# Gating and output projections of a decoder layer: five pairs of weight tiles by seven products in place of three, with weight sums made ahead in DRAM

## The chip, the core and the metric

The kernel runs on one core of one Trainium2 chip. TensorE (PE) multiplies, with weight loads (PEld) beside it; VectorE (DVE), ScalarE (ACT) and GpSimd (POOL) work on tiles in SBUF; SyncE (SP) and POOL issue the DMAs. The metric is the device time of one execution in microseconds.

## The reference

One decoder layer in float32 for 256 tokens (T) of width 2048 (D). Everything of size is a product of the 256 x 2048 activations with a weight matrix:

```python
h = RMSNorm_pre(x); p = h @ w_in    # columns: A (conv), B (spatial gate), C (attention), 3 x D merge gates
y = (g_A*A + g_B*B + g_C*C) @ w_o;  x = x + RMSNorm_post(y)
h = RMSNorm_pre(x); u = causal_dwconv3(h @ w_up)
x = x + RMSNorm_post((silu(u_g) * u_v) @ w_down)
```

The change touches the columns of `w_in` that give the third merge gate `g_C` ("gating", two blocks cp0 and cp1 of 1024 columns), and the first 1024 columns of `w_o` ("o").

## The kernel before, in words

A weight tile of 128 rows by 1024 columns is fetched by SP into one of five `wraw` buffers. ACT copies it, rounded, to `whi` (the "high part"), DVE subtracts to get `wlo` (the "low part"); each has a ring of four. Activations are kept as high and low parts too, 128 tokens by 128 rows. A product of an activation with 512 columns is three matmuls: high by high, high by low, low by high. So a plain tile (one k) takes two token halves x two column halves x 3 = 12 matmuls, and k runs over KT = 16 tiles of the 2048 rows.

In three places, gating cp0, gating cp1 and o, two k-tiles at a time are taken as a pair and multiplied by Strassen's scheme in Winograd's form: seven products in place of eight, from sums of the weights' four blocks and sums of the activations' four blocks. That is 21 matmuls in place of 24. `NG` is the number of such pairs per place, `REST` the plain k-tiles. `in_sevens` sets the order: two plain tiles, then the pairs with plain tiles between, then what plain tiles are left. `Seven.seven` makes the weight sums of a pair with half-tile operations on DVE (`tt` holds them), `Seven.combine` adds the side banks at the end. The activations' sums stand in `sh`; for gating they are made by `input_sums` from `hT` during the attention, for o by `sums4` from `mac`, transposed by PE (`pm`) in `mix_gen`.

The program has these stages, in this order: conv branch (`wf_a`), u, compressed keys (`kk`) and q projections; two branches (`branch`, four column blocks cb each) that form `mac`, with the attention worked off beside them; gating cp0, the C output `py` for cb 0 and 1, gating cp1, `py` for cb 2 and 3; o; the second half of the output projection; the feed-forward's up projection in 44 steps; the down projection in two halves (`Pair(0)`, `Pair(1)`) of 14 pairs and 16 plain tiles each. The down projection already takes weight sums that POOL makes ahead during the feed-forward, with DMAs from DRAM to DRAM, half of them adding into their target: two or four DMAs ("steps") a pair, 84 in all. Before the steps of a feed-forward step stands a copy of one column (`tick`) that makes POOL wait until the step's result is there.

The order of the work around the change is written out by hand: `fixed` chains operations on ACT and DVE each in the order of the code, `in_line` does so on PE; work outside these chains (attention, `mix_gen`, the adds to `mac`) is placed among them by the scheduler. In the down projection's second half, `keep` says after which pair a weight tile for the very end is prepared ahead into a buffer (`kept`) of the activations `gh` and `gl` that earlier pairs have read.

Of the kernel before, what the change touches and what calls it, by code (L numbers as in the profile page):

```python
# [43 lines left out]
NG, REST = 3, list(range(6, KT))  # L44
# [15 lines left out]
def block(ctx: ExitStack, tc: tile.TileContext, x, xf, fp, cst, rows, sgw, w1, w2, wf_a, wt_bv, wf_bu, wf_c,  # L60
# [473 lines left out]
    for j in range(8):  # L534
        pa = ftile(wf_a[2 * j], hT)
        sa = q1(f"sa{j}")
        fsum(pa, sa, rb=rb)
# [8 lines left out]
        pump(BUDGET)
# [44 lines left out]
    vbd = P1.tile([128, 2, 4, 128], F32, name="vbd")  # L591
# [280 lines left out]
    def input_sums(j):  # L872
# [3 lines left out]
        sums4(a[0], a[1], sh[:, j], f"h{j}")  # L876
        yield 0

    def attn():
# [3 lines left out]
        for n, u in enumerate(units):  # L883
# [3 lines left out]
            if n % 2 and n // 2 < NG:  # L887
                yield from input_sums(n // 2)
# [50 lines left out]
    class Seven:  # L939
# [23 lines left out]
        def seven(self, b, a, tt, acts, nm, last):  # L963

            L, U = slice(0, 512), slice(512, 1024)
            (hb, lb), (ha, la), (ht, lt), (h4, l4) = (ring(nm + x) for x in "bat4")
            high(hb, b)
            fixed(V, V.tensor_sub, tt[:, L], b[:, L], a[:, U])
            fixed(V, V.tensor_sub, a[:, U], a[:, U], a[:, L])
            high(ha, a)  # L970
            rest(lb, b, hb)
            fixed(V, V.tensor_sub, tt[:, U], b[:, L], a[:, U])
            high(ht, tt[:, 0:1024])
# [19 lines left out]
    def in_sevens(pr, plain, pairs, act, acts, tt, nm):  # L993
# [23 lines left out]
    def branch(bi, act_of):  # L1017

        for cb in range(4):
# [47 lines left out]
            for t in range(2):  # L1067
                for a in range(2):
                    cc = slice(cb * 512 + a * 256, cb * 512 + a * 256 + 256)
                    y = mac[:, t, cc] if bi == 0 else tgs[t, a]  # L1070
                    with tc.high_priority(offset=int(PR)):
                        V.scalar_tensor_tensor(y, tgs[t, a], 1.0, py[t][:, a * 256:a * 256 + 256], op0=ALU.add,
                                               op1=ALU.mult)
                        if bi:
                            V.tensor_add(mac[:, t, cc], mac[:, t, cc], y)
            pump(BUDGET)

    def mix_gen(cb):

        for j in range(2 * cb, 2 * cb + 2):  # L1080
# [10 lines left out]
            if j < NG:  # L1091
# [3 lines left out]
                mix["a", j] = a  # L1095
# [130 lines left out]
    def acts_m(j):  # L1226
        s1, s2, s4, s3 = parts(sh[:, j], range(4))
        return s4, m2(2 * j + 1, H1), m2(2 * j, H1), s1, s3, s2, m2(2 * j + 1, H2)

    in_sevens(po2, wt_op, wt_oq, m2, acts_m, tt, "o")  # L1230
# [179 lines left out]
    DR_seq = []  # L1410

    def pool_dma(*args, **kw):

        with ExitStack() as order:
            for ins in DR_seq:
                order.enter_context(tc.issue_after(ins))
            DR_seq[:] = [G.dma_start(*args, **kw).ins]  # L1417

    tick = PZ.tile([128, 1], F32, name="tick")
    ahead_of = {(p, j): DR.tile([128, 2 + n % 2, 512], F32, name=f"ahead{p}_{j}") for p in range(2)  # L1420
                for n, j in enumerate(TURNS[p])}
    away = [DR.tile([128, 2, 384], F32, name=f"away{j}") for j in range(AWAY)]

    def ahead_steps():

        late = deque()
        add = {"accum_op": ALU.add}
        for p in range(2):
            for n, j in enumerate(TURNS[p]):
                src, dst = wt_dq[p, j].rearrange("p (b n) -> p b n", b=4), ahead_of[p, j]  # L1430
                yield dst[:, 0:2], src[:, 2:4], {}
                if n % 2:
                    yield dst[:, 2], src[:, 0], {}
                while len(late) > 1 - n % 2:
                    yield late.popleft()
                late.append((dst[:, 0:2], src[:, 0:4:2], add))
                if n % 2:
                    late.append((dst[:, 2], dst[:, 1], add))
        yield from late

    steps = list(ahead_steps())
    count = len(steps)
    for i in range(NFT):
# [19 lines left out]
        for j, (k0, k1) in enumerate(PAIRS):  # L1463
            if i == k0:
                first = acc[0]
            elif i == k1:
# [3 lines left out]
                if j < AWAY:  # L1470
                    pool_dma(away[j], dst.rearrange("p x a b -> p x (a b)").bitcast(F32))
        with ExitStack() as order:
            for ins in DR_seq:
                order.enter_context(tc.issue_after(ins))
            DR_seq[:] = [G.tensor_copy(tick, g2(i, slice(0, 1))[0].bitcast(F32)).ins]
        while steps and len(steps) > count * (NFT - 2 - i) // (NFT - 2):
            dst, src, how = steps.pop(0)
            pool_dma(dst, src, **how)
# [15 lines left out]
    for j in TURNS[0][-AWAY:]:  # L1494
        pool_dma(home[:, j], away[j])
# [14 lines left out]
    class Pair(Seven):  # L1510
# [10 lines left out]
        def quad(self, n):  # L1521
# [3 lines left out]
            nm, last = f"q{self.p}_{j}", n == len(PAIRS) - 1  # L1525
            b = fetch(wt_dq[self.p, j][:, 0:1024], 1024)
            a = scratch()
            ahead = ahead_of[self.p, j]
            nc.sync.dma_start(a, ahead[:, 0:2].rearrange("p b n -> p (b n)"))
            r = fetch(wt_dq[self.p, j][:, 1536:2048], 512)  # L1530
            if n % 2:
                nc.sync.dma_start(r[:, 512:], ahead[:, 2])
            tt = fin[:, 7168:8192]
            s1, s2, s4 = summed_acts(j)
            L, U = slice(0, 512), slice(512, 1024)
            (hb, lb), (ha, la), (ht, lt), (hr, lr) = (ring(nm + x) for x in "batr")
            high(hb, b)
            if n % 2:
                rest(lb, b, hb)
                high(ha, a)  # L1540
                fixed(V, V.tensor_add, tt[:, L], b[:, U], r[:, U])
                rest(la, a, ha)
                high(hr, r)
                high(ht[:, L], tt[:, L])
                rest(lr, r, hr)
                rest(lt[:, L], tt[:, L], ht[:, L])
                six, four, one = ((hr, lr), U), ((ht, lt), L), ((hr, lr), L)
            else:
                fixed(V, V.tensor_add, tt[:, L], b[:, L], a[:, U])
                rest(lb, b, hb)  # L1550
                high(ha, a)
                fixed(V, V.tensor_add, tt[:, U], b[:, U], tt[:, L])
                rest(la, a, ha)
                high(ht, tt)
                high(hr[:, L], r[:, L])
                rest(lt, tt, ht)
                rest(lr[:, L], r[:, L], hr[:, L])
                six, four, one = ((ht, lt), L), ((ht, lt), U), ((hr, lr), L)
            todo = [(self.p6, s2, *six), (self.p1, g2(k0, H1), *one), (self.c[1][0], g2(k1, H2), *four)]
            side = (self.p1, self.p5, self.p6, self.p7)  # L1560
# [259 lines left out]
```

## Time and profile before

| what | value |
|---|---|
| runs | 1567.49, 1566.93, 1567.20 us; median 1567.2 |
| the profiled execution | 1566.37 us, span 1564.7, granted clock 0.998 |
| busy over the span | PE 1554.1, DVE 1284.4, ACT 925.3, POOL 112.7 us |
| conv, u, kk, q projections | 54 to 299 us |
| the two branches | 299 to 460, 460 to 622 |
| gating cp0, cp1 | 622 to 663, 686 to 728 |
| first half of the output projection | 751 to 794 |
| feed-forward, up | 840 to 1342 |
| down projection, two halves | 1342 to 1440, 1440 to 1555 |

All times are of one profiled execution on the one core, counted from the span's start. Busy time of PE overlaps: a matmul's row is longer than the distance to the next, since they are pipelined. The stages are read off the tiles that PE writes: `pg0a`, `pg1a`, `poa`, `pd0a`, `pd1a` and so on.

### The profile page before, as it was taken

What the parts mean: (1) busy time and instruction counts of PE and PEld (TensorE: products, weight loads), DVE (VectorE), ACT (ScalarE), POOL (GpSimd) and SP (SyncE); (2) the same over time, 40 slices, a digit from 0 to 9 for tenths busy, and PEclk for the clock granted to TensorE, in tenths of its full rate; (3) what the DMA queues carried; (4) which work ended last, traced back from release to release, by engine and by line L of the source; (5) the groups of instructions that cost most, each with busy time, mean ns of one, the idle gap of its engine ahead of it and who ended that gap; (6) DMA issues with size and microseconds to landing.
All of it is one profiled execution on the core that took longest, in us unless ns stands there. A gap on an engine that the chain in (4) does not pass through costs nothing.

```text
span 1564.7 us, 22800 instructions
## 1 busy us (share of the span) xinstructions
PE 1554.1 (99%) x8130; PEld 1320.0 (84%) x8130; DVE 1284.4 (82%) x2185; ACT 925.3 (59%) x1489; POOL 112.7 (7%) x182
## 2 busy tenths in 40 slices
PE   9999999999999999999999999999999999999998
PEld 7888889888887777888888888888888888888876
DVE  7899999978665554879887988888888777789997
ACT  7544544467487575556566656565555555566763
POOL 1000020000000000000000022122111121100000
PEclk9999999999999999999999999999999999999999
DMA  9555556657554546656684699889988899988793
GB/s 372 189 194 179 188 180 207 197 184 252 164 165 135 162 148 189 196 174 211 227 282 148 217 334 299 263 250 273 275 268 271 270 252 273 314 263 276 261 356 116
DMA packets 107442, 358.82 MB, mean 229 GB/s; under 512 B 11968, under 2 KB 13312, under 8 KB 106304
## 3 DMA queue, kind: packets, MB, share of 16 engines
q1 hardware_dynamic: 90144, 312.92, 60.2%
q0 software_dynamic: 16752, 44.05, 11.5%
q8 instruction: 63, 1.03, 0.3%
q10 hardware_dynamic: 432, 0.41, 0.1%
q14 instruction: 51, 0.42, 0.1%
HBM read 350.51 MB, written 42.47 MB: 251 GB/s over the span
## 4 chain that ended last, share of the span: by engine, by line
PE 97%; DVE 1%; ACT 1%; DMA 0%; issue 0%; DVEq 0%; SPq 0%; ACTq 0%
PE ps L178 29%; PE ps L185 15%; PE pd0b L953 5%; PE pg L199 4%; PE pg L200 4%; PE pg L198 4%; PE pd1a L953 3%; PE py L199 3%; PE py L198 3%; PE py L200 3%; PE pd0a L953 2%; PE pd1b L953 2%; PE poa L953 2%; PE pg1a L953 2%; PE pg0a L953 2%; PE po L198 1%
## 5 line engine op out<-in xcount | busy, mean ns | idle before, releaser
L150 DVE TENSOR_TENSOR wlo<-wraw,whi 128x1024 fp32r<-128x1024 f32 (+1 forms) x376 | 456.9, 1218 | 96.2 <-ACT whi L149 90.0
L149 ACT ACTIVATE whi<-wraw 128x1024 fp32r<-128x1024 f32 (+1 forms) x376 | 393.4, 1051 | 143.4 <-PE pg L200 42.0
L178 PE MATMUL ps<-h2T,whi 128*128 128x512 f32 x1360 | 325.0, 391 | 0.0
L178 PEld LDWEIGHTS ps<-h2T,whi 128*128 128x128 f32 x1360 | 249.8, 188 | 48.2
L185 PEld LDWEIGHTS ps<-h2T,wlo 128*128 128x128 f32 x1360 | 174.5, 191 | 6.7
L185 PE MATMUL ps<-h2T,wlo 128*128 128x256 f32 x1360 | 176.6, 283 | 0.0
L220 ACT ACTIVATE t<-ps 128x256 f32<-128x256 f32 x125 | 47.6, 382 | 186.3 <-PE ps L178 185.6
L178 PE MATMUL ps<-hT,whi 128*128 128x512 f32 x640 | 157.4, 392 | 0.0
L178 PEld LDWEIGHTS ps<-hT,whi 128*128 128x128 f32 x640 | 116.0, 188 | 21.3
L918 DVE TENSOR_TENSOR wlowraw<-wraw,whiwraw 128x1024 fp32r<-128x1024 f32 x74 | 89.7, 1223 | 34.1 <-ACT whiwraw L918 32.8
L481 DVE SCALAR_TENSOR_TENSOR cv<-hb,fps,cv 128x256 f32<-128x256 f32 x240 | 105.1, 479 | 0.2 <-ACT cv L477 0.2
L918 ACT ACTIVATE whiwraw<-wraw 128x1024 fp32r<-128x1024 f32 x74 | 77.8, 1058 | 46.3 <-PE py L200 16.5
L221 DVE TENSOR_TENSOR t<-ps,t 128x256 f32<-128x256 f32 x125 | 52.9, 424 | 63.3 <-ACT t L220 62.8
L200 PE MATMUL pg<-whi,hT 128*128 128x512 f32 x256 | 100.6, 393 | 0.0
L199 PE MATMUL pg<-wlo,hT 128*128 128x512 f32 x256 | 100.5, 393 | 0.0
L198 PE MATMUL pg<-whi,hT 128*128 128x512 f32 x256 | 98.7, 393 | 0.3 <-ACT mg L1042 0.3
L185 PEld LDWEIGHTS ps<-hT,wlo 128*128 128x128 f32 x640 | 84.7, 190 | 4.7
L185 PE MATMUL ps<-hT,wlo 128*128 128x256 f32 x640 | 86.8, 283 | 0.0
L199 PEld LDWEIGHTS pg<-wlo,hT 128*128 128x128 f32 x256 | 48.1, 188 | 10.4 <-issue 0.3
L200 PEld LDWEIGHTS pg<-whi,hT 128*128 128x128 f32 x256 | 48.1, 188 | 10.2 <-issue 0.7
L198 PEld LDWEIGHTS pg<-whi,hT 128*128 128x128 f32 x256 | 47.9, 188 | 10.0 <-ACT mg L1042 0.4
L1417 POOL DMA_DIRECT2D ahead<-in_wt_dq_dram x70 | 55.2, 814 | 6.5 <-DMA ahead<-in_wt_dq_dram 4.0
(1792 smaller groups left out, 2922.6 us busy)
## 6 DMA issues: line engine op xcount, KB each, us to landing
wraw<-in_wf_up_dram SPq DMA_DIRECT2D x176, 512.0 KB, 5.8
wraw<-in_wt_g_dram SPq DMA_DIRECT2D x64, 512.0 KB, 4.2
ahead<-in_wt_dq_dram POOLq DMA_DIRECT2D x56, 512.0 KB, 9.1
wraw<-in_wt_p_dram SPq DMA_DIRECT2D x48, 512.0 KB, 4.4
wraw<-in_wf_a_dram SPq DMA_DIRECT2D x32, 512.0 KB, 4.2
wraw<-in_wt_dn_dram SPq DMA_DIRECT2D x32, 512.0 KB, 4.8
wraw<-in_wt_dq_dram SPq DMA_DIRECT2D x28, 512.0 KB, 5.2
fin<-ahead SPq DMA_DIRECT2D x28, 512.0 KB, 5.1
```

Of the source, the lines that this page charges most:

```text
L149: S.activation(hi[:, :n], raw[:, :n], AF.Copy)
L150: V.tensor_sub(lo[:, :n], raw[:, :n], hi[:, :n].bitcast(F32))
L178: ins = PE.matmul(ps[:, :, ts], lhsT=ws[k // 8][0][:, c:c + 128], rhs=mov[:, k, :, ts], start=(k == 0 and not t), stop=(k == n - 1), skip_ ...
L185: ins = PE.matmul(ps[:, 1, ts], lhsT=ws[k // 8][1][:, c:c + 128], rhs=mov[:, k, 0, ts], start=False, stop=False, skip_group_check=True).ins
L198: PE.matmul(ps, lhsT=xh, rhs=hi, start=first, stop=False)
L199: PE.matmul(ps, lhsT=xh, rhs=lo, start=False, stop=False)
L200: return PE.matmul(ps, lhsT=xl, rhs=hi, start=False, stop=last).ins
L221: V.tensor_add(t1 if rb is not None else dst, ps[:, 0], t1)
L481: V.scalar_tensor_tensor(ca[:, j], hb[:, j, k:k + T], w(j, k), ca[:, j], op0=ALU.mult, op1=ALU.add)
L918: seq[eng] = [op(*args, **kw).ins]
L953: ins = PE.matmul(bank, lhsT=a[x], rhs=w[y], start=first and j == 0, stop=last and j == 2).ins
L1417: DR_seq[:] = [G.dma_start(*args, **kw).ins]
```

## The change

`NG` goes from 3 to 5 and `REST` from ten to six plain tiles, in all three places; between the pairs stand 0, 1, 0, 1, 0 plain tiles in place of 2, 2, 1. The pairs there now take their sums from DRAM in the way of the down projection, whose body becomes `Seven.seven`; the signs of the sums and of the final additions follow it. The 42 steps for these pairs stand first in a list of 126. `ahead_by` issues them: one after each of 8 conv, 8 u, 4 kk and 8 q tiles, and four after each column block of the two branches, 60 in all; 66 stay in the feed-forward. The activations' sums of pairs 3 and 4 get a buffer of their own, `sh2`; the fetched sums one of two halves, `qa` for gating and `oa` for o. In the last stage, `keep` is set after the pairs 5, 7, 11, 12 in place of 5, 7, 9, 11.

```diff
-NG, REST = 3, list(range(6, KT))
+NG, REST = 5, list(range(10, KT))
...
+    def ahead_steps():
+        quads = [(("g", cp, j), wt_gq[cp, j], j % 2) for cp in range(2) for j in range(NG)]
+        quads += [(("o", j), wt_oq[j], j % 2) for j in range(NG)]
+        quads += [((p, j), wt_dq[p, j], n % 2) for p in range(2) for n, j in enumerate(TURNS[p])]
+        for i, (key, _, six) in enumerate(quads):
+            made[key] = DR.tile([128, 2 + six, 512], F32, name=f"ahead{i}"), six
...
+        for key, src, six in quads:
+            src, dst = src.rearrange("p (b n) -> p b n", b=4), made[key][0]
+            yield dst[:, 0:2], src[:, 2:4], {}
+            if six:
+                yield dst[:, 2], src[:, 0], {}
+            while len(late) > 1 - six:
+                yield late.popleft()
+            late.append((dst[:, 0:2], src[:, 0:4:2], add))
+            if six:
+                late.append((dst[:, 2], dst[:, 1], add))
...
+    def ahead_by(mark, n):
+        pooled(G.tensor_copy, tick, mark)
+        for dst, src, how in steps[:n]:
+            pooled(G.dma_start, dst, src, **how)
+        del steps[:n]
...
+        ahead_by(hb[:, j, 30:31], 1)
...
+        ahead_by(ub[:, j, 0:1], 1)
...
+        ahead_by(kk[:, i % 2, i // 2, 0:1], 1)
...
+        ahead_by(qf[:, i, 0:1], 1)
...
+    for j in range(3, NG):
+        bg.append(input_sums(j))
...
-        def seven(self, b, a, tt, acts, nm, last):
+        def seven(self, quad, key, a, tt, acts, nm, last):
+            src, six = made[key]
+            b = fetch(quad[:, 0:1024], 1024)
+            nc.sync.dma_start(a, src[:, 0:2].rearrange("p b n -> p (b n)"))
+            r = fetch(quad[:, 1536:2048], 512)
+            if six:
+                nc.sync.dma_start(r[:, 512:], src[:, 2])
...
+            high(hb, b)
+            if six:
+                rest(lb, b, hb)
+                high(ha, a)
+                fixed(V, V.tensor_add, tt[:, L], b[:, U], r[:, U])
+                rest(la, a, ha)
+                high(hr, r)
+                high(ht[:, L], tt[:, L])
+                rest(lr, r, hr)
+                rest(lt[:, L], tt[:, L], ht[:, L])
...
+            else:
+                fixed(V, V.tensor_add, tt[:, L], b[:, L], a[:, U])
+                rest(lb, b, hb)
+                high(ha, a)
+                fixed(V, V.tensor_add, tt[:, U], b[:, U], tt[:, L])
+                rest(la, a, ha)
+                high(ht, tt)
+                high(hr[:, L], r[:, L])
+                rest(lt, tt, ht)
+                rest(lr[:, L], r[:, L], hr[:, L])
...
         for j in range(NG):
-            for _ in range((2, 2, 1)[j]):
+            for _ in range((0, 1, 0, 1, 0)[j]):
...
+            ahead_by(mac[:, 0, cb * 512:cb * 512 + 1], 4)
...
-                for j in range(NG):
-                    sums4(*mix["a", j], sh[:, j], f"m{j}")
+                for j in range(4):
+                    sums4(*mix["a", j], sh_of(j), f"m{j}")
...
-        keep = 1 if j in (5, 7, 9, 11) else 0
+        keep = 1 if j in (5, 7, 11, 12) else 0
```

How this moves instructions, at three places. First DVE at the start of o. Before, from the last C output's second low part (`wlowraw`) to the first pair's (`o0`) low parts:

```order
L918 TENSOR_TENSOR wlowraw_7119_7122<-wraw_7119,whiwraw_7119_7121 128x1024
L1155 SCALAR_TENSOR_TENSOR gates_6515<-gates_6515,py_6974 128x512
L1155 SCALAR_TENSOR_TENSOR gates_6515<-gates_6515,py_6975 128x512
L1156 TENSOR_TENSOR mac<-mac,gates_6515 128x512 x2
L918 TENSOR_TENSOR wlowraw_7137_7140<-wraw_7137,whiwraw_7137_7139 128x1024
L918 TENSOR_TENSOR tt<-wraw_7155,wraw_7157 128x512
L1088 SCALAR_TENSOR_TENSOR ml<-pm_6960,mh 128x512
L1088 SCALAR_TENSOR_TENSOR ml<-pm_6967,mh 128x512
L918 TENSOR_TENSOR wraw_7157<-wraw_7157 128x512
L918 TENSOR_TENSOR wloo0b<-wraw_7155,whio0b 128x1024
```

And after:

```order
L975 TENSOR_TENSOR wlowraw_7316_7319<-wraw_7316,whiwraw_7316_7318 128x1024
L975 TENSOR_TENSOR tt<-wraw_7346,oa 128x512
L975 TENSOR_TENSOR wloo0b<-wraw_7346,whio0b 128x1024
L925 TENSOR_TENSOR sh_5030<-sqm_7103,sh_5030 128x256
L1237 SCALAR_TENSOR_TENSOR gates_6704<-gates_6704,py_7200 128x512
L1237 SCALAR_TENSOR_TENSOR gates_6704<-gates_6704,py_7201 128x512
L975 TENSOR_TENSOR tt<-wraw_7346,tt 128x512
L975 TENSOR_TENSOR wloo0a<-oa,whio0a 128x1024
L1164 SCALAR_TENSOR_TENSOR ml<-pm_7172,mh 128x512
L1164 SCALAR_TENSOR_TENSOR ml<-pm_7193,mh 128x512
L1238 TENSOR_TENSOR mac<-mac,gates_6704 128x512 x2
L918 TENSOR_TENSOR spm_7183<-ma_7180,ma_7179 128x128
```

The additions to `mac` (L1156, now L1238) stood right behind `gates`; now two half-tile sums, a low part and both `ml` stand ahead of them, and the sums of pair 4's activations (`spm`) follow.

Second, ACT in the last stage, around pairs 9 and 0 of the down projection's second half. Before:

```order
L918 ACTIVATE whiq_9t<-fin 128x512
L918 ACTIVATE whiwraw_14688_14690<-wraw_14688 128x1024
L918 ACTIVATE kept_14706<-wraw_14707 128x1024
L918 ACTIVATE whiq_0b<-wraw_14711 128x1024
L918 ACTIVATE whiq_0a<-fin 128x1024
```

After, from the same pair on, and two pairs later:

```order
L975 ACTIVATE whiq_9t<-fin 128x512
L975 ACTIVATE whiwraw_14879_14881<-wraw_14879 128x1024
L975 ACTIVATE whiq_0b<-wraw_14897 128x1024
L975 ACTIVATE whiq_0a<-fin 128x1024
...
L975 ACTIVATE whiq_1t<-fin 128x512
L975 ACTIVATE whiwraw_14991_14993<-wraw_14991 128x1024
L975 ACTIVATE kept_15009<-wraw_15010 128x1024
L975 ACTIVATE whiq_2b<-wraw_15014 128x1024
```

The kept tile behind pair 9 is gone from there and stands behind pair 1; DVE's order has the same move.

Third, POOL's queue in the first branch. Before, the paddings of `bt` (the attention's compressed keys) stand one behind the other:

```order
L608 MEMSET bt_3536 128x16
L608 MEMSET bt_3579 128x16
L608 MEMSET bt_3855 128x16
L608 MEMSET bt_3860 128x16
L608 MEMSET bt_3865 128x16
```

After:

```order
L653 MEMSET bt_3643 128x16
L653 MEMSET bt_3686 128x16
L122 COPY tick<-mac 128x1
L122 DMA ahead_79<-in_wt_oq_dram 128x1024
L122 DMA ahead_78<-in_wt_oq_dram 128x2x512
L122 DMA ahead_80<-in_wt_oq_dram 128x1024
L122 DMA ahead_80<-in_wt_oq_dram 128x512
L653 MEMSET bt_3967 128x16
L653 MEMSET bt_3972 128x16
```

Between the two halves' paddings now stand a wait for `mac`'s second column block and four issues.

More of the change, by code (lines that the diff above doesn't have):

```diff
@@ L64, in block @@
     V, S, PE, G = nc.vector, nc.scalar, nc.tensor, nc.gpsimd
+    DR = ctx.enter_context(tc.tile_pool(name="dram", bufs=1, space=bass.MemoryType.DRAM))
     PZ = ctx.enter_context(tc.tile_pool(name="pz", bufs=1))
@@ L112, in block, with pooled @@
     fetched = [None]
+    in_pool = []
+    def pooled(op, *args, **kw):
+        with ExitStack() as order:
+            for ins in in_pool:
+                order.enter_context(tc.issue_after(ins))
+            in_pool[:] = [op(*args, **kw).ins]
+    tick = PZ.tile([128, 1], F32, name="tick")
+    made = {}
+    def ahead_steps():
[4 more added lines that the diff above has]
+            made[key] = DR.tile([128, 2 + six, 512], F32, name=f"ahead{i}"), six
+        late = deque()
+        add = {"accum_op": ALU.add}
+        for key, src, six in quads:
[8 more added lines that the diff above has]
+                late.append((dst[:, 2], dst[:, 1], add))
+        yield from late
+    steps = list(ahead_steps())
+    def ahead_by(mark, n):
[3 more added lines that the diff above has]
+        del steps[:n]
     def split2(raw):
@@ L590, in block @@
     kcb = P1.tile([128, 2, 32], F32, name="kcb")
-    vbd = P1.tile([128, 2, 4, 128], F32, name="vbd")
+    vbd = P1.tile([128, 2, 4, 128], F32, tag="vbd", name="vbd")
     kd_t = s8([128, 2, 4, T], F32, "kd")
@@ L855, in values, with sh_of @@
             yield 650
-    sh = P1.tile([128, NG, 2, 4, 128], R, name="sh")
+    sh = P1.tile([128, 3, 2, 4, 128], R, name="sh")
+    sh2 = []
+    def sh_of(j):
+        if j >= 3 and not sh2:
+            sh2.append(s8([128, 2, 2, 4, 128], R, "sh2"))
+        return sh[:, j] if j < 3 else sh2[0][:, j - 3]
     H1, H2 = slice(0, 128), slice(128, T)
@@ L886, in attn @@
             yield from u.weights()
-            if n % 2 and n // 2 < NG:
+            if n % 2 and n // 2 < 3:
                 yield from input_sums(n // 2)
@@ L965, in seven @@
             L, U = slice(0, 512), slice(512, 1024)
-            (hb, lb), (ha, la), (ht, lt), (h4, l4) = (ring(nm + x) for x in "bat4")
+            (hb, lb), (ha, la), (ht, lt), (hr, lr) = (ring(nm + x) for x in "batr")
             high(hb, b)
[L968 to L973, printed above, removed]
@@ L991, in combine, with total, in_sevens @@
             fixed(V, V.tensor_add, self.at(1, 0), self.p7, self.at(1, 0))
-    def in_sevens(pr, plain, pairs, act, acts, tt, nm):
+        def total(self, n):
+            return V.tensor_sub if n else V.tensor_add
+    def in_sevens(pr, plain, pairs, act, acts, keys, spare, tt, nm):
         todo = [(k, weights(plain[REST.index(k)])) for k in REST[0:2]]
@@ L998, in in_sevens @@
         for j in range(NG):
-            for _ in range((2, 2, 1)[j]):
+            for _ in range((0, 1, 0, 1, 0)[j]):
                 k = rest_.pop(0)
                 pr.k_tiles([(k, weights(plain[REST.index(k)]))], act)
-            b, a = (fetch(pairs[j][:, x:x + 1024], 1024) for x in (0, 1024))
-            pr.seven(b, a, tt, acts(j), f"{nm}{j}", j == NG - 1)
+            pr.seven(pairs[j], (*keys, j), spare(j), tt, acts(j), f"{nm}{j}", j == NG - 1)
         for k in rest_:
@@ L1109, in hx, with acts_of @@
         return hT[:, k, 0, ts], hT[:, k, 1, ts]
-    def acts_h(j):
-        s1, s2, s4, s3 = parts(sh[:, j], range(4))
-        return s4, hx(2 * j + 1, H1), hx(2 * j, H1), s1, s3, s2, hx(2 * j + 1, H2)
+    def acts_of(j, x):
+        s1, s2, s4, s3 = parts(sh_of(j), range(4))
+        return s4, x(2 * j + 1, H1), s3, s1, s2, x(2 * j + 1, H2), x(2 * j, H1)
     def wp(cb, k):
@@ L1121, in block @@
         gates = s8([128, 2, 2, 512], F32, f"gates{cp}")
+        pump(1e6)
         if cp == 0:
-            tt = s8([128, 2048], F32, "tt")
-        pump(1e6)
+            tt = P1.tile([128, 1024], F32, tag="vbd", name="tt")
+            qa = s8([128, 2, 1024], F32, "qa")
         pr = Seven([PS.tile([128, 512], F32, tag="acc", name=f"pg{cp}a{i}") for i in range(4)],
@@ L1131, in block @@
             for t in range(2):
-                fixed(V, V.tensor_add, gates[:, t, n], pr.c[t][n], gates[:, t, n])
+                fixed(V, pr.total(n), gates[:, t, n], pr.c[t][n], gates[:, t, n])
                 fixed(S, S.activation, gates[:, t, n], gates[:, t, n], AF.Tanh, scale=rh[:, t:t + 1])
@@ L1224, in m2 @@
         return mh[:, k, ts], ml[:, k, ts]
[L1226 to L1230, printed above, removed]
+    oa = P0.tile([128, 2, 1024], F32, tag="hT", name="oa")
+    in_sevens(po2, wt_op, wt_oq, m2, lambda j: acts_of(j, m2), ("o",), lambda j: oa[:, j % 2], tt, "o")
     for n in range(2):
@@ L1408, in kept_sums @@
         return (se, sf)[j % 10 // 5][:, :, j % 5]
[L1410 to L1421, printed above, removed]
-    away = [DR.tile([128, 2, 384], F32, name=f"away{j}") for j in range(AWAY)]
[L1424 to L1441, printed above, removed]
+    away = [DR.tile([128, 2, 384], F32, name=f"away{j}") for j in range(AWAY)]
     count = len(steps)
@@ L1470, in block @@
                 if j < AWAY:
[L1471 to L1478, printed above, removed]
+                    pooled(G.dma_start, away[j], dst.rearrange("p x a b -> p x (a b)").bitcast(F32))
+        ahead_by(g2(i, slice(0, 1))[0].bitcast(F32), max(0, len(steps) - count * (NFT - 2 - i) // (NFT - 2)))
     P2b_ctx.close()
@@ L1494, in block @@
     for j in TURNS[0][-AWAY:]:
-        pool_dma(home[:, j], away[j])
+        pooled(G.dma_start, home[:, j], away[j])
     def summed_acts(j):
@@ L1524, in quad @@
             k0, k1 = PAIRS[j]
[L1525 to L1533, printed above, removed]
-            s1, s2, s4 = summed_acts(j)
@@ L1535, in quad @@
[L1535 to L1558, printed above, removed]
@@ L1559, in quad @@
-            todo = [(self.p6, s2, *six), (self.p1, g2(k0, H1), *one), (self.c[1][0], g2(k1, H2), *four)]
-            side = (self.p1, self.p5, self.p6, self.p7)
-            for bank_, act, (h, l), c in (
-                    (self.c[0][1], s4, (hb, lb), L), (self.c[0][0], g2(k1, H1), (hb, lb), U),
-                    (self.p7, g2(k0, H2), (ha, la), L), (self.p5, s1, (ha, la), U),
-                    *(todo if n % 2 else [todo[0], todo[2], todo[1]])):
-                in_line(self.mm, bank_, act, (h[:, c], l[:, c]), last and any(bank_ is x for x in side))
@@ L1578, in at @@
+            self.seven(wt_dq[self.p, j], (self.p, j), scratch(), fin[:, 7168:8192],
+                       (s4, g2(k1, H1), g2(k0, H2), s1, s2, g2(k1, H2), g2(k0, H1)), f"q{self.p}_{j}",
+                       n == len(PAIRS) - 1)
         def at(self, t, n):
```

42 lines of the change are left out of this document (17 added, 25 removed).

## The prediction

> **What bounds the kernel now.** I read the page first: engine shares, then the chain of waits.
>
> ```profile
> PE 1554.1 (99%) x8130; PEld 1320.0 (84%) x8130; DVE 1284.4 (82%) x2185; ACT 925.3 (59%) x1489; POOL 112.7 (7%) x182
> PE 97%; DVE 1%; ACT 1%; DMA 0%; issue 0%; DVEq 0%; SPq 0%; ACTq 0%
> ```
>
> The chain runs through PE for 97% of the span, so a matmul removed is time removed, if what feeds PE keeps up. What one costs is read from the chain inside the first gating projection (start, length, count):
>
> ```profile
> 622.08 12.25 PE pg0a L953 x54
> 634.32 2.74 PE pg0b L953 x12
> 637.06 7.49 PE pg0a L953 x33
> ```
>
> That is 12.25 / 54 = 0.227 us per matmul of 512 columns. Single rows of the same matmul (below) read 0.39 us; they overlap, and pricing by them would almost double the gain. Next the stages (stretch, length, then busy time of PE, PEld, DVE, ACT, POOL, granted clock, DMA share, GB/s):
>
> ```profile
> 54.00:110.00 56.00, 56.00 (x324) 49.49 (x323) 54.00 (x100) 30.47 (x42) 0.00 (x0) 1.00 0.60 195
> 110.00:226.00 116.00, 116.00 (x675) 102.45 (x674) 113.90 (x224) 56.12 (x84) 8.46 (x16) 1.00 0.57 183
> 226.00:262.00 36.00, 36.00 (x261) 34.82 (x260) 35.62 (x67) 16.69 (x24) 0.00 (x0) 1.00 0.71 213
> 460.00:622.00 162.00, 162.00 (x793) 124.92 (x792) 84.99 (x180) 105.95 (x233) 0.57 (x1) 1.00 0.52 159
> 622.00:664.00 42.00, 42.00 (x187) 34.72 (x186) 36.52 (x47) 22.57 (x25) 0.00 (x0) 1.00 0.60 192
> 750.00:794.00 44.00, 44.00 (x203) 36.45 (x202) 39.60 (x49) 24.39 (x27) 1.08 (x2) 1.00 0.68 236
> 864.00:1342.00 478.00, 478.00 (x2738) 421.96 (x2737) 399.09 (x698) 282.79 (x464) 91.96 (x132) 1.00 0.90 271
> 1342.00:1440.00 98.00, 98.00 (x434) 81.16 (x433) 85.99 (x93) 65.69 (x69) 2.59 (x5) 1.00 0.87 289
> 1440.00:1509.00 69.00, 69.00 (x306) 57.13 (x305) 64.46 (x70) 47.74 (x56) 0.00 (x0) 1.00 0.83 283
> ```
>
> PE is full in each, and DVE is the engine nearest behind it. The third gating projection is the two stretches 622 to 664 and a twin at 686; 750 to 794 is the first half of the output projection.
>
> **Part 1: fewer matmuls.** A plain pair of weight tiles takes 24 matmuls, a pair by seven products 21. Two more pairs in each of three places: 3 x 2 x 3 = 18 fewer (the order has 4189 rows on PE before, 4171 after), 18 x 0.227 = **-4.1 us**, 1.4 us per place.
>
> **Part 2: DVE in those places.** Prices (busy sum, mean ns):
>
> ```profile
> L918 DVE TENSOR_TENSOR wlowraw<-wraw,whiwraw 128x1024 fp32r<-128x1024 f32 x9 | 10.8, 1221 | 2.4 <-ACT whiwraw L918 2.2
> L918 DVE TENSOR_TENSOR tt<-wraw,wraw 128x512 f32<-128x512 f32 x6 | 4.1, 684 | 0.0
> ```
>
> A pair before: 3.5 low parts and four half-tile sums, 3.5 x 1.22 + 4 x 0.68 = 7.0. After, with sums from DRAM: two half-tile sums, 5.6, or one, 5.0. A place goes from 10 x 1.22 + 3 x 7.0 = 33.2 to 6 x 1.22 + 3 x 5.6 + 2 x 5.0 = 34.1: +0.9. Gating: 36.52 + 0.9 = 37.4 in 40.6 us, 92%. The last stretch of the table runs the same cadence of pairs (two, then a plain tile) at 64.46 / 69 = 93% DVE with PE full, so I cost this at 0. The output half also gets the activation sums of one more pair (four 128x128 and two 128x256 additions, by the tile sizes an estimate of 2 us): 39.60 + 0.9 + 2 = 42.5 in 42.6. That has no cover in the stretch itself; the stretch's end is additions that PE doesn't wait for. Bounds 0 and +3 (all of it exposed); beyond the start (part 3) I take 0, as the row nearest in cadence had no wait. The sums of pairs 3 and 4 for gating (by the same sizes an estimate of 6 us) lie in 460 to 622, where DVE idles 77 us.
>
> **Part 3: start of the output half.** The order puts the last additions to mac behind the first pair's work on DVE; PE's second group of transposes (pm) reads mac.
>
> ```profile
> 750.12 1.28 DVE L1155 SCALAR_TENSOR_TENSOR gates<-gates,py 128x512 f32<-128x512 f32 x2
> 751.32 1.29 DVE L1156 TENSOR_TENSOR mac<-mac,gates 128x512 f32<-128x512 f32 x2
> 752.52 1.22 DVE L918 TENSOR_TENSOR wlowraw<-wraw,whiwraw 128x1024 fp32r<-128x1024 f32 x1
> 753.66 0.68 DVE L918 TENSOR_TENSOR tt<-wraw,wraw 128x512 f32<-128x512 f32 x1
> 754.26 1.28 DVE L1088 SCALAR_TENSOR_TENSOR ml<-pm,mh 128x512 fp32r<-128x512 f32 x2
> ...
> 756.11 0.38 PE L1085 MATMUL pm<-idn,mac 128*128 128x128 f32 x2
> ```
>
> Before, mac was ready at 752.6 and that group began at 756.11. Pitches by start to start: two of 512 columns 1.20, a low part 1.14, one half-tile 0.60. After, counted from the last product of py: the second plain tile's low part ends at -1.0 (an estimate; bounds -1.0 and +0.3), then tt 0.6, low part 1.14, sum 0.35, gates 1.20, tt 0.6, low part 1.14, ml 1.20, mac 0.6 and 0.6: 5.8 and 6.4. PE gets there after 22 matmuls and the first pm group, 22 x 0.227 + 0.9 = 5.9. Between -0.1 and +0.5 by this ledger, up to 1.8 with the other bound: stall **+0.4 us**.
>
> **Part 4: the kept tile in the last stage.** The change also moves where weights 12 and 13 of the down projection's end are prepared ahead (after n = 11 and 12 instead of 9 and 11).
>
> ```profile
> 1509.44 1.06 ACT L918 ACTIVATE kept<-wraw 128x1024 fp32r<-128x1024 f32 x1 [2.06 <-PE pd1a L953]
> 1510.54 1.23 DVE L918 TENSOR_TENSOR kept<-wraw,kept 128x1024 fp32r<-128x1024 f32 x1 [1.86 <-ACT kept L918]
> ...
> 1512.19 0.39 PE L953 MATMUL pd1a<-whiq_0b,home 128*128 128x512 f32 x1
> 1512.28 1.22 DVE L918 TENSOR_TENSOR wloq_0b<-wraw,whiq_0b 128x1024 fp32r<-128x1024 f32 x1
> ...
> 1513.55 0.50 PE L953 MATMUL pd1a<-wloq_0b,home 128*128 128x512 f32 x1 [0.98 <-DVE wloq_0b L918]
> ...
> 1515.63 0.39 PE L953 MATMUL pd1b<-whiq_0a,gl 128*128 128x512 f32 x1
> ```
>
> ACT waits 2.06 us for PE before it may write kept over an activation that pair 9 still reads; DVE and then PE wait behind it. From 1512.19 to 1515.63 eight matmuls take 3.44 us instead of 8 x 0.2276 = 1.82: 1.6 lost. Two pairs later that buffer's reader is done. The kept tile of n = 12 then adds 1.2 us on DVE ahead of the last pair, which has room:
>
> ```profile
> 1531.60 1.22 DVE L918 TENSOR_TENSOR wloq_3b<-wraw,whiq_3b 128x1024 fp32r<-128x1024 f32 x1
> ...
> 1536.55 0.39 PE L953 MATMUL pd1a<-wloq_3b,home 128*128 128x512 f32 x1
> ```
>
> 3.7 us lie between. So **-1.6 us** (bounds -1.6 and 0).
>
> **Part 5: 60 sum steps issued early by POOL** (one beside each of 28 tiles, 4 per column block of the two branches; 18 fewer in the feed-forward). Prices of a fetch, a step's landing, and POOL's issue:
>
> ```profile
> wraw<-in_wf_up_dram SPq DMA_DIRECT2D x161, 512.0 KB, 5.8
> ahead<-in_wt_dq_dram POOLq DMA_DIRECT2D x56, 512.0 KB, 9.1
> wraw<-in_wt_gq_dram SPq DMA_DIRECT2D x4, 512.0 KB, 3.9
> L1417 POOL DMA_DIRECT2D ahead<-in_wt_dq_dram x70 | 55.2, 814 | 6.5 <-DMA ahead<-in_wt_dq_dram 4.0
> ```
>
> The feed-forward takes 84 steps in 490 us at 271 GB/s with PE full, fetches landing in 5.8 instead of 3.9; five buffers of 2.73 us of PE each (12 x 0.2276) are 13.7 us of cover. So 0 for the 28 spaced like that (5.6 to 11 us apart). In the three places the fetched volume rises from 16 tiles of 512 KB (10 plain, two for each pair) to 19.5 (6, and two and a half or three for each pair), 252 GB/s over 40.6 us, under the 289 above: 0. POOL's queue: the paddings of bt for the second half now stand behind a tick on mac and four issues:
>
> ```profile
> 371.54 1.41 DVE L1072 SCALAR_TENSOR_TENSOR mac<-mg,py 128x256 f32<-128x256 f32 x4
> 374.02 1.41 ACT L615 ACTIVATE bk<-bt 128x256 fp32r<-128x256 f32 x4
> ```
>
> First mac at about 371.9, then 4 x 0.81: 375.1, so ACT's bk may be 1.1 us late; bounds 0 and +1.1, taken 0, as ACT then waits for PE anyway.
>
> The tick itself, a GpSimd copy, now runs beside DVE stretches that are 96 to 99% full (54 to 262, 4.5 us idle together; 20 ticks):
>
> ```profile
> L1475 POOL COPY tick<-gh x44: 236/867/1497, 878.5 to 1342.0; 128x1 f32<-128x1 f32 x44
> L150 DVE TENSOR_TENSOR wlo<-wraw,whi 128x1024 fp32r<-128x1024 f32 x165 | 201.8, 1223 | 5.9 <-ACT whi L149 1.7
> L150 DVE TENSOR_TENSOR wlo<-wraw,whi 128x1024 fp32r<-128x1024 f32 x30 | 36.5, 1217 | 0.4 <-ACT whi L149 0.2
> ```
>
> The tick lasts 0.24 to 1.50 us, longer by about one low part: it waits. DVE's low part is 6 ns longer with POOL at work (165 rows of the feed-forward) than without (30 rows of 54 to 133): 1 us on half of DVE's work, 2 us per 44 ticks, 0.9 us for 20, less than the 4.5. So 0. [...]
>
> **Sum.** -4.1 - 1.6 + 0.4 = -5.3. The profiled execution took 1566.37 (span 1564.7), 0.8 under the median of 1567.2; so 1561.1 for it and **1561.9** for the median. Its own bounds: 1561.5 with no stall at the start to 1563.3 with 1.8.
>
> **Rivals.**
> - The kept tile's move gains nothing, because the wait moves to another tile or the spilled rows' return, now later in SP's queue, binds: 1567.2 - 3.7 = 1563.5. For it: it is a wait among many on two engines; against: the 3.7 us room.
> - DVE becomes the bound of the output half, and at smaller size of gating's second stretch: 2 to 4 us of wait there, 1563.9 to 1565.9. For it: 42.5 of 42.6; against: the 93% stretch without a wait.
> - Slower: in the branches four steps go out back to back, eight times. One burst reads and writes 4.2 MB. If SP's fetches were served behind it at the 271 GB/s of the feed-forward, they would come 15.5 us late against 13.7 of cover: 8 x 1.8 = +14.4, 1576. It decides from about 285 GB/s down (1.05 us over the cover, eight times, is 8.4 us). Against: fetches beside single steps lost only 1.9 us, and these stretches move 159 GB/s.
> - Ticks hold DVE: 20 x 0.87 = 17.4 - 4.5 idle = +12.9, 1575. The 6 ns speak against it.
>
> **How the numbers follow.** Forecast 0.63, kept tile 0.10, DVE 0.16, bursts 0.08, ticks 0.03. About 0.2% (3.1 us) can be told from no change: faster below 1564.1, slower above 1570.3. Faster: 0.63 + 0.10 + 0.01 of the DVE case = 0.74; same 0.15; slower 0.11. The range takes the first three cases, 1560.7 (the sum's lower bound less the 0.8 between execution and median) to 1566.5.
>
> **What would show it.** Right: gating stretches of 40.6 us each without a PE wait; no wait for wloq_0b in the last stage; a PE wait under 1 us before the second pm group. Wrong: PE waits on DVE low parts from the third pair of the output half on; fetches in the branches landing over 8 us with ACT waiting for them; low parts over 1.3 us in 54 to 262.

## The result and the profile after

Slower: 1578.2 us (median of 1577.6, 1577.8, 1578.6 and 1579.8) against 1567.1 of the kernel before, ratio 1.0072, interval [1.0055, 1.009], that is 0.7% and clear of no change. The forecast was 1561.9, so 16.3 us are to be found. The profiled execution, the slowest of the four, took 1579.84 us, span 1577.8, 13.1 more than before. The page of the changed kernel, its first line and its chain:

```profile
PE 1556.2 (99%) x8112; PEld 1318.3 (84%) x8112; DVE 1295.0 (82%) x2213; ACT 938.8 (59%) x1513; POOL 159.5 (10%) x260
PE 87%; DVE 6%; DMA 3%; ACT 2%; issue 1%; ACTq 0%; DVEq 0%; SPq 0%
```

PE has 18 matmuls fewer and still 2.1 us more busy time, and the chain, 97% PE before, is 87% PE. PE's waits (what waited for what, us, times, longest), of which the kernel before had none over 1.0 us between its first matmuls and its tail, are below. The view counts a wait from the end of the matmul before. Counted from start to start it is 0.15 to 0.2 us longer; where the text says 3.8 for the first, and 4.0 for the two of `poa` together, it counts so.

```profile
PE pg1b L1010 <- ACT ma L1170: 3.6, 1, 3.6
...
PE poa L1010 <- DVE ml L1164: 2.4, 1, 2.4
PE kcp L697 <- DMA w2s<-in_w_dram: 1.8, 1, 1.8
...
PE poa L1010 <- ACT mh L1163: 1.3, 1, 1.3
PE py L242 <- DVE wlowraw L975: 0.9, 2, 0.7
PE pd1a L1010 <- DVE wloq_2b L975: 0.6, 1, 0.6
```

Three of them stand at the starts of cp1 and of o. The same stages in both kernels, from PE's first matmul of each (columns as in the prediction's table); before, gating cp0 with its C output, cp1, its C output, o:

```profile
622.10:686.40 64.30, 64.30 (x289) 53.21 (x289) 52.23 (x64) 34.69 (x39) 0.00 (x0) 1.00 0.63 199
686.40:728.60 42.20, 42.20 (x191) 34.93 (x190) 37.58 (x45) 24.05 (x30) 0.00 (x0) 1.00 0.56 182
728.60:750.40 21.80, 21.80 (x97) 17.99 (x97) 18.81 (x34) 12.79 (x19) 0.00 (x0) 1.00 0.66 210
750.40:793.80 43.40, 43.40 (x200) 35.98 (x199) 39.00 (x47) 24.39 (x27) 1.08 (x2) 1.00 0.68 235
```

After; here the C output's stretch holds the 2.4 us from its last product to o's first (a pm group and a wait), and the last two rows are the 4 us that begin about where the two long waits end:

```profile
622.40:688.20 65.80, 65.54 (x291) 52.38 (x290) 54.02 (x65) 37.56 (x42) 3.61 (x5) 1.00 0.79 248
688.20:735.00 46.80, 43.16 (x186) 35.14 (x185) 37.27 (x43) 27.74 (x36) 0.59 (x1) 0.96 0.63 202
735.00:760.00 25.00, 23.20 (x105) 18.71 (x104) 23.17 (x45) 16.14 (x24) 1.06 (x2) 1.00 0.71 240
760.20:805.90 45.70, 43.35 (x185) 35.24 (x186) 39.05 (x49) 26.71 (x32) 0.00 (x0) 0.96 0.69 229
701.00:705.00 4.00, 3.93 (x11) 3.11 (x12) 0.46 (x1) 1.95 (x5) 0.00 (x0) 0.61 0.38 125
763.00:767.00 4.00, 3.74 (x9) 2.99 (x10) 3.07 (x9) 1.05 (x4) 0.00 (x0) 0.57 0.96 380
```

Each place should be 1.4 us shorter. cp1 is 4.6 longer; o, from the end of the C output (757.8), took 48.1 in place of 43.4, 4.7 longer; the C output between, without those 2.4 us, 1.0; cp0 with its output 1.5, of which 1.9 are attention matmuls that stood ahead of 622 before. So 11.8 of the 13.1 us lie between 622 and 806. Gating began 0.3 later although that attention work had moved behind it, and from 806 to the end the kernel took 1.0 longer.

**cp1, row by row** (PE, DVE and ACT of the changed kernel):

```profile
696.61 0.82 PE L1161 MATMUL pm<-idn,mac 128*128 128x128 f32 x6
699.64 1.28 DVE L1164 SCALAR_TENSOR_TENSOR ml<-pm,mh 128x512 fp32r<-128x512 f32 x2
700.35 1.25 ACT L1170 ACTIVATE ma<-pm 128x256 f32<-128x256 f32 x4 [1.52 <-DVE ml L1164]
701.07 0.51 PE L1010 MATMUL pg1b<-whig10t,sh 128*128 128x512 f32 x1 [3.65 <-ACT ma L1170]
```

The transposes of mac's second column block (pm) stand in a PSUM bank of the same ring as the four side banks of the pairs. The first pair's fifth product (`whig10t`) needs that bank, and DVE and ACT have not yet read it. In the kernel before, the same pm group ran at 694.79 and the same product at 700.70, without a wait: two more plain tiles, 5.5 us, stood ahead of the first pair.

```profile
694.79 0.81 PE L1085 MATMUL pm<-idn,mac 128*128 128x128 f32 x6
700.70 0.39 PE L953 MATMUL pg1b<-whig10t,sh 128*128 128x512 f32 x1
```

In o of the changed kernel:

```profile
757.84 1.04 PE L1161 MATMUL pm<-idn,mac 128*128 128x128 f32 x8
759.05 1.07 ACT L1163 ACTIVATE mh<-pm 128x512 fp32r<-128x512 f32 x2
760.17 0.50 PE L1010 MATMUL poa<-whiwraw,mh 128*128 128x512 f32 x1 [1.30 <-ACT mh L1163]
761.93 1.28 DVE L1164 SCALAR_TENSOR_TENSOR ml<-pm,mh 128x512 fp32r<-128x512 f32 x2
763.26 0.79 PE L1010 MATMUL poa<-whiwraw,ml 128*128 128x512 f32 x1 [2.35 <-DVE ml L1164]
```

With pairs on k = 0 to 9, the first plain tiles are k = 10 and 11 in place of 6 and 7. Their activations are transposed only here, and the low part ml is 5.4 us behind the end of the C output.

### The profile page after: what moved, and what is told of

It is laid out like the page before. It is cut to its first block, busy times and chain, and to the rows that moved or that the text cites. A ratio compares the mean times of both kernels' runs of the same rounds, so it can differ in the third digit from the quotient of the medians.

```text
span 1577.8 us, 23019 instructions
## 1 busy us (share of the span) xinstructions
PE 1556.2 (99%) x8112; PEld 1318.3 (84%) x8112; DVE 1295.0 (82%) x2213; ACT 938.8 (59%) x1513; POOL 159.5 (10%) x260
## 4 chain that ended last, share of the span: by engine, by line
PE 87%; DVE 6%; DMA 3%; ACT 2%; issue 1%; ACTq 0%; DVEq 0%; SPq 0%
PE ps L221 29%; PE ps L228 15%; PE pd0b L1010 4%; PE pg L241 3%; PE pg L242 3%; PE pg L243 3%; PE pd0a L1010 2%; PE py L242 2%; PE py L243 2%; PE py L241 2%; PE pd1a L1010 2%; PE poa L1010 2%; PE pg0a L1010 2%; PE pg1a L1010 2%; PE pd1b L1010 1%
## 5 line engine op out<-in xcount | busy, mean ns | idle before, releaser
L975 DVE TENSOR_TENSOR wlowraw<-wraw,whiwraw 128x1024 fp32r<-128x1024 f32 x62 | 75.1, 1222 | 28.4 <-ACT whiwraw L975 27.5
L975 ACT ACTIVATE whiwraw<-wraw 128x1024 fp32r<-128x1024 f32 x62 | 64.8, 1057 | 33.1 <-PE py L243 7.5
L122 POOL COPY tick<-gh 128x1 f32<-128x1 f32 x44 | 31.3, 712 | 367.1 <-ACT gh L1509 367.1
L242 PEld LDWEIGHTS pg<-wlo,hT 128*128 128x128 f32 x256 | 48.1, 188 | 10.6 <-issue 0.7
L243 PEld LDWEIGHTS pg<-whi,hT 128*128 128x128 f32 x256 | 48.1, 188 | 10.1 <-issue 0.3
```

Of the source, the lines that this page charges most:

```text
L242: PE.matmul(ps, lhsT=xh, rhs=lo, start=False, stop=False)
L243: return PE.matmul(ps, lhsT=xl, rhs=hi, start=False, stop=last).ins
L975: seq[eng] = [op(*args, **kw).ins]
```

## The experiments

Experiments 1 to 4, 5 to 8 and 9 to 11 are three groups; the kernels of one group ran on one chip together with the kernel before, each group on another chip. Where a ratio is given, it is to the kernel before of that group, and the interval behind it says how sure it is.

**1. The kept tiles alone, in the kernel before**

```diff
-        keep = 1 if j in (5, 7, 9, 11) else 0
+        keep = 1 if j in (5, 7, 11, 12) else 0
```

> The kernel before with only the moved kept tiles (after the pairs 5, 7, 11, 12). Theory 1, the wait moves: the 1.6 us behind pair 9 go, and as in the changed kernel about 1.0 us appears at the low part of pair 2, so -0.6, about 1566.5 against 1567.1. Rival (the prediction): the whole 1.6 is won, 1565.5. Rival 2: the new place costs as much as the old, 1567.

Measured 1566.1 against 1567.6: 0.9991 [0.9982, 1.0], -1.4. The trace has no wait in the last stage ahead of its tail, and PE's second half of the down projection took 109.9 us in place of 111.7. So the prediction's -1.6 stands nearer than theory 1, though the interval holds both. The wait of 0.6 us for `wloq_2b` in the changed kernel goes back to a fetch (the chain there):

```profile
1527.52 10.22 DMA wraw<-in_wt_dq_dram
```

The traces of experiments 2 to 4, with the same move, don't have this wait; that of experiment 8 has it again (0.5).

**2. Gating: the first pair two plain tiles later**

```diff
-            for _ in range((0, 1, 0, 1, 0)[j]):
+            for _ in range(counts[j]):            # gating (2, 0, 1, 0, 0), o as it was
```

> The changed kernel with other plain tiles between the gating pairs (2, 0, 1, 0, 0 in place of 0, 1, 0, 1, 0), so that the first pair comes two plain tiles, 5.5 us of PE, later. Theory 1: the wait of 3.8 us in the first pair of cp1 is for the PSUM bank in which the transposed mac still stands, and 1.6 us more are the half clock behind it; both go, 1578.2 - 5.4 = 1572.8. Rival: the pairs are too dense for DVE; three pairs without a plain tile between then wait about as long later, 1577 to 1580.

Measured 1578.4, ratio 1.0072 [1.0059, 1.0084]: no gain. The wait for the bank is gone and cp1 took 41.4 us in place of 46.8, but the C outputs now wait for DVE:

```profile
PE py L242 <- DVE wlowraw L975: 5.2, 4, 1.6
```

Its stretches of cp1 and of the C output behind:

```profile
690.40:731.80 41.40, 41.40 (x187) 34.02 (x185) 34.61 (x41) 27.13 (x35) 0.59 (x1) 1.00 0.72 223
731.80:757.30 25.50, 22.67 (x98) 17.85 (x97) 23.67 (x45) 14.23 (x21) 0.00 (x0) 1.00 0.66 224
```

Both theories were half right: the wait was the bank, and three pairs without a plain tile between push their DVE work into the next stage. There DVE is busy 23.67 of 25.5 us, with the activations' sums for o on top. In the changed kernel DVE is as busy there (23.17 of 25.0 us), but PE's waits for it in the C outputs are only 0.9 us; that this load is also what makes ml late in o is argued, not shown.

**3. The output half: other k-tiles as pairs**

```diff
+OJ, REST_O = [0, 1, 2, 4, 5], [6, 7, 12, 13, 14, 15]     # pairs k = 2j, 2j + 1, and plain tiles, of o
```

> The changed kernel with other k-tiles as pairs in the output half only: pairs from k 0 to 5 and 8 to 11, plain 6, 7, 12 to 15, so that the first two plain tiles need activations (6, 7) that are ready long before, as in the kernel before. Theory 1: the output half waits 4.0 us at its start because its first plain tiles are now k = 10 and 11, whose transposes come out of the third column block, and 1.9 us more are the half clock behind; 1578.2 - 5.8 = 1572.4. Rival: the wait comes from DVE, which has two more pairs' activation sums to make there; here two pairs' sums stand in the start of the output half instead of one, so it stays or grows, 1578 to 1580.

Measured 1573.2, 1.0039 [1.0026, 1.0053]: 5.0 us under the changed kernel (by the ratios 5.2). The waits for mh and ml are gone; of o's stall there remains one of 1.4 us, again for a bank that holds pm, and behind it no slow matmuls (0.23 us apart from the second on):

```profile
PE pg1b L1011 <- DVE ml L1165: 3.6, 1, 3.6
...
PE pob L1011 <- ACT ma L1171: 1.4, 1, 1.4
```

**4. Two early steps per column block in place of four**

```diff
-            ahead_by(mac[:, 0, cb * 512:cb * 512 + 1], 4)
+            ahead_by(mac[:, 0, cb * 512:cb * 512 + 1], 2)
```

Here the last addition to the sums of o's fifth pair is issued only after o has read them, so that pair is multiplied by incomplete sums; the work is the same.

> The changed kernel with two sum steps per column block of the branches instead of four (16 go back to the feed-forward). Theory 1: a burst of four holds up the fetch of w2s, for which PE waits 1.8 us at 379; half the burst, and the wait is under 0.5: 1578.2 - 1.5 to 2 = 1576.4. Rival: the burst is not the cause, the wait stays, 1578.

Measured 1577.9, 1.0071 [1.0058, 1.0083]. In its trace the wait for w2s is gone, while one of 1.1 us stands at the first q tile (0.3 in the changed kernel's trace). In the changed kernel, w2s was issued at 372.80 and a burst of four steps at 373.33, and w2s took 8.3 us. But in experiment 8, whose kernel issues the same burst 0.53 us after w2s, w2s took 5.4 us and PE did not wait for it, nor does it in the traces of 5, 6 and 9 with four steps a block. So the burst alone does not make the wait; what does stays open, and a gain in time is not shown.

**5. The form alone: three pairs in the old order, with sums from DRAM**

```diff
-NG, REST = 5, list(range(10, KT))
+NG, REST = 3, list(range(6, KT))
...
-            for _ in range((0, 1, 0, 1, 0)[j]):
+            for _ in range((2, 2, 1)[j]):
```

> The changed kernel with three pairs and ten plain tiles again in the three places (2, 2, 1 plain tiles between), but the pairs' weight sums still from DRAM, made early. Theory 1: the loss comes from more pairs in the same order, not from the sums' new form; the kept tiles give -1.5, the early steps cost the 2 us seen before 622: 1567.6. Rival: the form itself (its fetches, its order on ACT and DVE) brings the waits at the starts of cp1 and o, then they are still there and the time is above 1572.

Measured 1567.0, ratio 1.0 [0.9991, 1.0009]; no PE wait between 622 and 850. So neither the sums from DRAM nor their 60 early steps bring the waits; with the kept tiles' -1.4 in the result, they cost about 1.4 together, by the two intervals anything from nothing to about 3.4.

**6 and 7. Four pairs in cp1, o's tiles as in 3; then fewer early steps**

```diff
+NG1, REST1 = 4, list(range(8, KT))           # cp1: plain tiles (2, 1, 1, 1) between; o as in 3
...
-        ahead_by(kk[:, i % 2, i // 2, 0:1], 1)    # 7 only; and three steps per column block
```

> The changed kernel with the output half's pairs and plain tiles as in e3_o_tiles, and in gating cp1 four pairs with the order 2, 1, 1, 1 of plain tiles, so that the first pair comes later and the pairs are not dense at the end. Theory 1: against e3_o_tiles (1573.2) the bank wait of cp1 and its half clock go (-5.7), one pair less costs 0.7: 1568.2. Rival: DVE's load moves the wait into the C output behind, as in e2_gating_order: 1573.

> e6_four_pairs with the early steps spread otherwise: none beside the kk tiles (226 to 262, where the DMA engines are 92% busy), three instead of four per column block of the branches. Theory 1: the waits for the first q tile's fetch and for w2s, together some 2 us, shrink by half or more: 1 to 2 us under e6_four_pairs. Rival: they don't depend on the number of steps, the same as e6_four_pairs within 0.5.

Measured 1570.2, 1.0018 [1.0009, 1.0027], and 1569.4, 1.0012 [1.0004, 1.0021]. In 6 the bank wait of cp1 is gone (cp1 took 41.7 us as far as the last product), but part of it is back as DVE's lateness in the C outputs:

```profile
PE py L244 <- DVE wlowraw L977: 2.4, 3, 1.2
PE pob L1012 <- ACT ma L1172: 1.5, 1, 1.5
```

So of the 5.0 us expected 3.0 came. Between 6 and 7 gating began 1.3 us earlier in the traces; the times differ by 0.8 with overlapping intervals, so this stays open. The trace of 6 has no wait for w2s, and 0.3 at the first q tile: the 2 us that the expectation for 7 meant to win were not there.

**8. Zero matmuls in the wait of cp1** (`zz` is a tile of zeros)

```diff
+                if key == ("g", 1, 0) and bank_ is todo[0][0]:
+                    for _ in range(16):
+                        in_line(lambda: PE.matmul(self.c[0][0], lhsT=zz, rhs=hb[:, L], start=False, stop=False).ins)
```

> The changed kernel with 16 matmuls of a zero tile, adding nothing, in PE's order in the wait of 3.8 us in cp1's first pair. Theory 1: the matmuls behind the wait run at half speed because PE stood still, so with PE at work the wait's length stays (3.6 us of zeros, 0.2 to 0.4 of wait) and the slow matmuls are gone: 0.23 us pitch behind it, 1578.2 - 1.6 = 1576.6. Rival: they are slow because of what ACT and DVE do at that time, or of the data's lateness; then the pitch behind it stays at 0.43 and the time at 1578.

Measured 1576.6, 1.0061 [1.0048, 1.0074]: -1.6, the number of theory 1. This interval overlaps with the changed kernel's, so the time alone does not show it; the trace does: cp1 took 45.1 us in place of 46.8, 1.7 less. The rows at the same place:

```profile
695.21 3.75 PE L1061 MATMUL pg1a<-whig10b,zz 128*128 128x512 f32 x15
698.79 0.40 PE L1013 MATMUL pg1b<-whig10t,sh 128*128 128x512 f32 x1
699.03 0.40 PE L1013 MATMUL pg1b<-wlog10t,sh 128*128 128x512 f32 x1
```

And the 4 us behind the bank's release, which had a clock of 0.61:

```profile
698.70:702.70 4.00, 4.00 (x20) 3.26 (x19) 2.61 (x3) 3.19 (x4) 0.00 (x0) 1.00 0.28 107
```

The wait is filled, the bank comes no earlier (12.8 us behind cp1's first product, 12.9 in the changed kernel), and the matmuls behind start every 0.23 us in place of 0.43.

**9. Five pairs in cp0 alone** (cp1 and o with three, as in 5)

```diff
+NG1, REST1, C1, CO = 3, [6, 7, 8, 9, 10, 11, 12, 13, 14, 15], (2, 2, 1), (2, 2, 1)
+OJ, REST_O = [0, 1, 2], [6, 7, 8, 9, 10, 11, 12, 13, 14, 15]
```

> e5_form_alone (three pairs, sums from DRAM) with five pairs in gating cp0 alone, in the changed kernel's order 0, 1, 0, 1, 0. Theory 1: cp0 has no transposes of mac standing in its side banks, so five pairs cost nothing there and gain their 6 matmuls, 1.4 us, less the 0.4 of a late low part in the C output behind: 1566.97 - 1.0 = 1566.0. Rival: DVE is what pairs lack, wherever they stand; then waits show in cp0 or its C output and the time is 1567 or more.

Measured 1565.7, 0.9991 [0.9982, 1.0], 1.2 under experiment 5, which ran on another chip and whose interval [0.9991, 1.0009] overlaps with this one. The only PE wait from 622 to 850 is the forecast one:

```profile
PE py L244 <- DVE wlowraw L977: 0.3, 1, 0.3
```

**10. Five, three and four pairs**

```diff
+NG1, REST1, C1, CO = 3, [6, 7, 8, 9, 10, 11, 12, 13, 14, 15], (2, 2, 1), (2, 1, 1, 1)
+OJ, REST_O = [0, 1, 2, 5], [6, 7, 8, 9, 12, 13, 14, 15]
...
-            ahead_by(mac[:, 0, cb * 512:cb * 512 + 1], 4)
+            ahead_by(mac[:, 0, cb * 512:cb * 512 + 1], 2)
```

> Five pairs in cp0, three in cp1 in the old order, four in the output half with the first two pairs of plain tiles k = 6 to 9 ahead and one plain tile behind each pair; two early steps per column block. Theory 1: none of these places meets a bank with transposes in it nor a late transpose, so the 9 matmuls fewer than three pairs each are won (-2.0), and fewer steps cost less ahead of 622 (-0.5): 1564.5 to 1565.5, under the kernel before. Rival: the pairs' sums on DVE in the C output of cp1 make waits there again: 1567.

Measured 1565.3, 0.9989 [0.998, 0.9998]: under both kernels. The 1.7 us under experiment 5 agree with the 9 matmuls (-2.0) and the wait of 0.3, though these intervals overlap too. Against the kept tiles alone (0.9991) it can't be told apart.

**11. Experiment 5 without the steps in the branches** (`ahead_by` with 0 steps there)

> e5_form_alone without the early steps of the branches (28 early steps in place of 60). Theory 1: the bursts of four cost about 1.1 us there (gating began at 623.0 in place of 621.9), which comes back: 1565.9. Rival: the bursts cost nothing that can be measured, 1567.0.

Measured 1566.1, 0.9995 [0.9986, 1.0004]: 0.9 under experiment 5, within the intervals. Its trace has gating begin at 623.0 as well, so the place that the expectation named is not it. What the early steps cost, about 1 us or nothing, stays open.

## Why the prediction was wrong

- **Part 1 held.** 0.227 us a matmul is what experiments 9 and 10 agree with, within their intervals, and cp1 in experiment 2 (41.4 us where 40.8 were due).
- **Part 2 failed** at "the row nearest in cadence had no wait", from which it took 0. That row, the down projection's second half, has no transposes in its banks, and its first pair comes 8.2 us behind its first product (1442.8 to 1451.0); in the changed cp1 it is 5.4 (688.2 to 693.6), before 11.8. cp1 and o begin with transposes in banks of that ring, and with gates, mac, ml and sums still to do on DVE and ACT. Bringing the first pair forward by two plain tiles took away the 5.5 us in which those were read: 3.8 us of wait in cp1 and 1.6 of slow matmuls behind (the wait is gone in experiment 2, the slow matmuls in 2 and 8). Density, which the part did ask about, cost 0.4 and 0.8 in the C outputs.
- **Part 3 failed by its reader.** Its ledger has ml end 5.2 us after the C output (the trace: 5.4), but asked only when mac would be there for the second pm group. The first plain tile reads ml too, of k = 10 now, and PE would have come to it 1.4 us after the C output, behind the pm group and two matmuls: 4.0 us of wait and 1.7 of slow matmuls, where +0.4 was taken. The wait that it did forecast, before the second pm group, did not come.
- **Part 4 held in the kernel before** (experiment 1: -1.4 measured, -1.6 forecast, with an interval that reaches 0). In the changed kernel's trace the second half of the down projection took 111.2 us in place of 111.7, so only 0.5 of it was won there.
- **Part 5** took 0. The changed kernel's trace has 1.8 us of wait for w2s, 0.3 at the first q tile, and about 1.0 at the down projection's first pair, where a fetch of sums from DRAM landed late (`fin<-ahead`, 8.97 us from issue to landing; DVE stood 4.06 us for it). The first two are not steady: the trace of experiment 8, with the same early steps, has neither. The burst rival had eight bursts at 1.8; at most one met a transfer that PE waited for. The ticks' rival fell, as no run shows a tick that holds DVE: DVE's low parts between 54 and 262 are as long after as before (1216 and 1218 ns), while the ticks beside u take up to 1.56 us:

```profile
L193 DVE TENSOR_TENSOR wlo<-wraw,whi 128x1024 fp32r<-128x1024 f32 x70 | 84.9, 1216 | 2.9 <-ACT whi L192 2.5
```

```profile
L122 POOL COPY tick<-ub x8: 183/690/1555, 162.4 to 206.2; 128x1 f32<-128x1 f32 x8
```

- **The size.** In the profiled execution the span came out at +13.1 where -5.3 was forecast, 18.4 apart: cp1 6.0, o 5.7, cp0 1.0 and the C output behind cp1 1.0, 2.2 ahead of 622 (0.2 in the trace of experiment 8, so most of it is not steady), and 2.6 behind 806 (1.0 at the first pair of the down projection, 1.0 by the fetch in experiment 1, the rest not traced). The rival "DVE becomes the bound" named o, but as a matter of its throughput and at 2 to 4 us; no rival had a bank.

## What to carry to other kernels

When tiles are exchanged between two forms, ask of each first reader in a stage what it reads and whether that exists yet: which k the first plain tile now has, and which bank the first pair now needs. Throughput over a whole stage, even at 93% without a wait in a twin, says little about its first 10 us, where the last stage's left-overs are read. A product moved forward in PE's order takes its cover away from everything behind which it used to stand.

## What the hardware showed

The waits at the starts of cp1 and of o cost more than their length. Behind the wait of 3.6 us in cp1, and behind those of 1.3 and 2.4 us with two matmuls between them in o, eight matmuls (cp1) and six (o) started every 0.43 us, at the granted clocks of 0.61 and 0.57 shown above, and then every 0.23 again: 1.6 and 1.7 us more. In cp1 the first three behind the wait still kept the old pitch. Behind single waits of up to 1.6 us (experiments 2, 3 and 6) the pitch was 0.23 from the second matmul on. The step down and the step back, in cp1 of the changed kernel:

```profile
701.64 0.43 PE L1010 MATMUL pg1b<-whig10t,sh 128*128 128x512 f32 x1
701.88 0.63 PE L1010 MATMUL pg1a<-whig10t,hT 128*128 128x512 f32 x1
702.30 0.63 PE L1010 MATMUL pg1a<-wlog10t,hT 128*128 128x512 f32 x1
...
703.58 0.63 PE L1010 MATMUL pg1b<-wlog10r,hT 128*128 128x512 f32 x1
704.01 0.63 PE L1010 MATMUL pg1b<-whig10r,hT 128*128 128x512 f32 x1
...
704.86 0.59 PE L1010 MATMUL pg1a<-wlowraw,hT 128*128 128x512 f32 x1
705.29 0.39 PE L1010 MATMUL pg1a<-whiwraw,hT 128*128 128x512 f32 x1
```

Experiment 8 ties it to PE standing still: with zeros multiplied in the wait of cp1, the clock stayed at 1.00; in o, where nothing filled the waits, that was not tried. The slow stretches are 3.4 us long in cp1 (701.88 to 705.29) and 3.5 in o (763.26 to 766.79): the two shorter waits of o, close together, had about the same behind them as the one of cp1. What sets the length of such a stretch no run here shows. In this kernel a stall of 3.6 us, whole or in two parts, is to be priced with 1.6 to 1.7 us on top; where between 1.6 and 3.6 us of waiting that begins, no run here shows.
